# Branch gates of a streaming-encoder layer on a seven-product scheme, woven into the mixer

## The chip, the cores and the metric

The kernel runs on one core of one Trainium2 chip. A core has a matrix engine (TensorE, "PE"; "PEld" is its weight loading), a vector engine (VectorE, "DVE"), an activation engine (ScalarE, "ACT"), GpSimd ("POOL") and a queue that only issues transfers (SyncE, "SP"). Each works through its own list of instructions in order, and semaphores tie the lists together. The metric is the device time of one execution in microseconds.

## The reference, cut to what matters

One layer: a SwiGLU feed-forward part, a normalisation, a mixer, a normalisation, a second feed-forward part, a normalisation, and a gated embedding. There are 256 rows (positions) of 2048 channels, all float32. The change is in the mixer:

```python
proj = x @ w_in                                  # (256, 2048) @ (2048, 11272)
mq, mk, mv, mo, mi, mf, sq, sk, sv, ga, gb = _split_cols(proj)
...                                              # mLSTM branch -> y_m, stick-breaking branch -> y_sb
merged = sigmoid(ga) * (y_m @ w_up_m) + sigmoid(gb) * (y_sb @ w_up_sb)
return merged @ w_out
x = _layer_norm(ALPHA * x + mix, ln2_g, ln2_b)   # the residual x is needed again here
```

`ga` and `gb` are 2048 columns each. In blocks of 512 columns there are four pairs (ga block g, gb block g), g = 0 to 3.

## The kernel before, in words

**Products.** Float32 products are made of three reduced ones. Every weight tile of 256 rows by 512 columns ("raw") is loaded by SP's queue (line 997), rounded by ACT into a high part (line 1024), and DVE makes the low part as the difference (line 1028). Activations are kept transposed and split in the same way. A *unit* multiplies one weight tile by the activations of one half of the rows (128 positions): for each of two 128-row slices hi*hi, hi*lo and lo*hi (lines 1073 to 1075), so six matmuls of 512 columns. In the plain form (`group`) a weight tile serves two units, one for each half of the rows.

**The seven-product scheme** (`seven`, used by `up7` in both feed-forward parts). Two column blocks A and B with the same inputs, two halves of the rows and two halves of each 512-row chunk form 2 x 2 blocks, which are multiplied with seven products in place of eight, after Winograd's variant of Strassen's scheme. Each product needs a tile of its own, some of them sums of weight blocks. In the feed-forward parts one sum is made while loading, by an accumulating transfer on POOL's queue (line 1001), the others on DVE (line 310). The activations' sums ("forms") are made by `form_turn`. The results are combined on DVE (line 463). Products 1 and 2 run first (four units each); then for each of four chunks one unit of products 5, 7, 6, 4 and 3, so that these five accumulators are open together.

**Order of the work.** The program is one list of units, written by hand; `weave` mixes a side list evenly into a main list. A small planner keeps a clock that advances with each unit's six matmuls (0.2161 us each); all other work (transposes, normalisation, attention heads) are generators that are put into the engines' lists when their due time has come (`DELAY`). Loads and splits are put in ahead of the units: up to 8 raw tiles in the feed-forward parts and 5 in the mixer, and 6 split tiles (`limits`, `loads`, `split_one`, `splits_due`). In SBUF there is one pool of 44 pages of 4 KB per partition for everything large, and beside it the residual `xres` (two tiles of 8 KB per partition). In PSUM there are 8 banks, in one pool for accumulators ("mm") and for short-lived results ("ms").

**The mixer.** The columns of `w_in` come in groups: query, key, gates, value, output gate (mLSTM), then the 24 stick-breaking columns of 128 (`sb_columns`, six groups, the last with 256 columns), then the branch gates (`branch`, evicted by ACT with the sigmoid) and the up products (`ups`; DVE multiplies each result by its gate, line 861, and adds the two branches, line 864). Order: gates 0 and 1, ups 0 and 1, gates 2, ups 2, gates 3, ups 3. `merge_turn` transposes the merged result; those of g = 0 to 2 are due 1 to 6 us after the gates of 3.

**Stick-breaking heads** (`stick`). Eight heads run as two sequences, so that two heads go side by side, in four waves. Each head has three phases, and each of them takes a bank: scores (lines 791 on), cumulative sums (line 804, read by DVE in line 806), and the product with the values (line 814, read by ACT and DVE, lines 243 and 244). Between the phases are planner delays of 6.6 and 6.7 us (s0, s1) and of 5.0 us (s2).

Of the kernel before, what the change touches and what calls it, by code (L numbers as in the profile page):

```python
# [13 lines left out]
P = 128  # L14
# [11 lines left out]
PAGES = 44  # L26
# [3 lines left out]
RAW_FFN, RAW_MIX, RAW_EDGE = 8, 5, 4  # L30
SPLIT_FFN, SPLIT_MIX, SPLIT_EDGE = 6, 6, 11
# [14 lines left out]
    "alpha": 24.0, "form": 18.0, "ln_turn": 3.6, "ln_step": 2.1, "gb": 14.0, "h": 8.0, "silu": 6.0, "late": 9.0, "rest": 1.2, "mt": 3.2,  # L46
# [46 lines left out]
class ActT:  # L93


    def __init__(self, alloc, forms=None):
        self.alloc = alloc
        self.forms, self.whole = forms, {}
        self.tiles = {}
        self.left = {}  # L100
# [39 lines left out]
class Boundary:  # L140


    def __init__(self, mixer):
        self.mixer = mixer
# [25 lines left out]
def kernel(  # L170
# [12 lines left out]
    res_pool = ctx.enter_context(tc.tile_pool(name="res", bufs=1))  # L183
# [49 lines left out]
    xres = [res_pool.tile([P, D], F32, name=f"xres{t}") for t in range(TT)]  # L233

    def load_x(c, t):
        cs = slice(c * COL, (c + 1) * COL)
        nc.sync.dma_start(out=xres[t][:, cs], in_=x[t * P:(t + 1) * P, cs])
# [8 lines left out]
    def transposed(src, act, c, t):  # L246
# [5 lines left out]
        if act.forms:  # L252
# [5 lines left out]
        if act.forms and all(act.ready(c, h) for h in range(TT)):  # L258
            sched.spawn(form_turn(act, c), DELAY["form"] + 5.0 * c)
# [17 lines left out]


# [16 lines left out]
    def seven(wa, wb, rows, col0, cols, act, done):  # L295
# [19 lines left out]
        for m, sub in ((1, 0), (2, 2)):  # L315
            for i in range(n):
                units.append(unit(m, i, plain(rows_of(wa, (4 * i + sub) * P, col0, cols)), act, 0, sub))
        for i in range(n):
            b11, b12, b22, b21 = (rows_of(w, (4 * i + sub) * P, col0, cols)
                                  for w, sub in ((wa, 0), (wb, 0), (wb, 2), (wa, 2)))  # L320
            t1 = Raw(b12.src, cols, b11.src)
            t3, add = (Raw(b12.src, cols, b22.src), None) if i == n - 1 else (b12, plus(b12, b12, b22))
            first = Weight(t1, [t1], [])
            units += [
                unit(5, i, first, act.forms, 0, 0),
                unit(7, i, Weight(t3, [t3, b22], [t3], add), act.forms, 1, 0),
# [5 lines left out]

    program = []

    def boundary(mixer):
        program.append(Boundary(mixer))


    class Norm:
        def __init__(self, g, b, act, scale, wait):  # L340
            self.g_in, self.b_in, self.act, self.scale, self.wait = g, b, act, scale, wait
# [769 lines left out]
```

## Time and profile before

| what | value |
|---|---|
| median of 3 runs | 2207.58 us (2207.19 to 2207.64) |
| profiled execution | 2207.09 us |
| span of the profile | 2205.4 us |
| granted TensorE clock | 1.00 |
| busy, PE / DVE / ACT / POOL | 2196.6 / 1747.1 / 1244.5 / 118.9 us |
| read from memory | 539.90 MB |

How to read the rows shown below: in a row of a group the first number after the bar is the busy time in us, the second the mean duration of one in ns, and after the second bar stands the engine's idle time before these instructions with what ended it. Rows of instructions begin with start and duration in us. Rows of stretches give for each engine the busy time and the number of instructions, then the granted clock, the share of the DMA engines and GB/s. Matmuls are pipelined: their durations overlap, and the rate is read from their starts. The slices of the page are 55 us each: 0 to 12 are the first feed-forward part, 13 to 25 the mixer, 26 to 37 the second feed-forward part.

### The profile page before, as it was taken

The numbers are of one execution on the slowest core, as the hardware profiler recorded it, in microseconds if no ns is written. First come the engines' busy times: TensorE is split into PE (matmuls) and PEld (weight loads), VectorE is DVE, ScalarE is ACT, GpSimd is POOL, SyncE is SP. The second block draws the span as 40 slices with busy tenths as digits, with TensorE's granted clock in tenths as the row PEclk, the third lists the DMA queues.
The fourth block names the chain that finished last, engine by engine and source line by source line (L and its number), as shares of the span: only waits on it lengthen the run. The fifth ranks groups of instructions, "written<-read, shape, count | busy, mean of one in ns | idle before, by whom it ended". The sixth has DMA issues, their size and how long they took to land.

```text
span 2205.4 us, 27919 instructions
## 1 busy us (share of the span) xinstructions
PE 2196.6 (100%) x10062; PEld 1819.0 (82%) x10062; DVE 1747.1 (79%) x1923; ACT 1244.5 (56%) x1505; POOL 118.9 (5%) x111
## 2 busy tenths in 40 slices
PE   9999999999999999999999999999999999999999
PEld 7888888888888888888888888888888888887888
DVE  6999999999987874654445456699999999989774
ACT  7556656565655555545643344656565565656372
POOL 0100010000000000000100000000010001000000
PEclk9999999999999999999999999999999999999999
DMA  9899999999993765655566666579989999999553
GB/s 334 246 312 299 283 283 318 303 308 275 320 315 115 217 199 158 190 164 167 158 190 187 187 225 218 183 230 303 303 265 306 324 287 298 288 301 336 200 165 104
DMA packets 284811, 543.85 MB, mean 247 GB/s; under 512 B 17120, under 2 KB 26240, under 8 KB 284672
## 3 DMA queue, kind: packets, MB, share of 16 engines
q1 hardware_dynamic: 262912, 500.12, 68.3%
q0 software_dynamic: 21760, 41.95, 11.0%
q8 instruction: 79, 1.29, 0.2%
q14 instruction: 60, 0.49, 0.1%
HBM read 539.90 MB, written 2.10 MB: 246 GB/s over the span
## 4 chain that ended last, share of the span: by engine, by line
PE 94%; DVE 2%; DMA 2%; issue 1%; ACT 0%; SPq 0%; DVEq 0%; POOLq 0%; ACTq 0%
PE mm L1074 30%; PE mm L1073 30%; PE mm L1075 30%; DMA raw<-in_ffn_w_dram 2%; DVE split L1028 1%; PE ms L249 1%; PE ms L392 0%; DVE raw L310 0%; PE ms L791 0%; PE ms L814 0%; PE ms L742 0%; PE ms L754 0%; PE ms L804 0%; ACT split L1024 0%; DVE actT L256 0%
## 5 line engine op out<-in xcount | busy, mean ns | idle before, releaser
L1028 DVE TENSOR_TENSOR split<-raw,split 128x1024 fp32r<-128x1024 f32 (+1 forms) x1013 | 1177.6, 1201 | 237.8 <-ACT split L1024 225.3
L1024 ACT CAST split<-raw 128x1024 fp32r<-128x1024 f32 (+1 forms) x1013 | 1007.0, 1036 | 496.9 <-DVE raw L310 139.5
L1073 PE MATMUL mm<-split,actT 128*128 128x512 f32 (+2 forms) x3152 | 1226.9, 389 | 0.5 <-DVE xres L516 0.5
L1074 PE MATMUL mm<-split,actT 128*128 128x512 f32 (+2 forms) x3152 | 1215.1, 386 | 1.4 <-DVE split L1028 1.3
L1075 PE MATMUL mm<-split,actT 128*128 128x512 f32 (+2 forms) x3152 | 1215.1, 386 | 0.6 <-DVE actT L256 0.6
L1074 PEld LDWEIGHTS mm<-split,actT 128*128 128x128 f32 x3152 | 592.8, 188 | 120.3 <-DVE split L1028 6.1
L1075 PEld LDWEIGHTS mm<-split,actT 128*128 128x128 f32 x3152 | 592.2, 188 | 121.0 <-DVE actT L256 1.4
L1073 PEld LDWEIGHTS mm<-split,actT 128*128 128x128 f32 x3152 | 592.6, 188 | 117.0 <-issue 1.0
L310 DVE TENSOR_TENSOR raw<-raw 128x1024 f32<-128x1024 f32 x176 | 214.6, 1219 | 1.9
L1001 POOL DMA_DIRECT2D raw<-in_ffn_w_dram x80 | 95.9, 1198 | 1415.7 <-DMA raw<-in_ffn_w_dram 404.1
L251 ACT CAST actT<-ms 128x512 fp32r<-128x512 f32 x60 | 35.0, 585 | 89.4 <-PE ms L249 88.4
L463 DVE TENSOR_TENSOR temp<-mm,temp 128x512 f32<-128x512 f32 x112 | 76.7, 685 | 6.4 <-PE mm L1075 4.6
L516 DVE SCALAR_TENSOR_TENSOR xres<-mm,xres 128x512 f32<-128x512 f32 x96 | 65.3, 684 | 15.9 <-PE mm L1075 15.8
L256 DVE TENSOR_TENSOR actT<-ms,actT 128x512 fp32r<-128x512 f32 x60 | 40.9, 683 | 24.6 <-ACT actT L251 13.7
L221 ACT ACTIVATE big<-mm 128x512 f32<-128x512 f32 x20 | 12.0, 598 | 55.8 <-PE mm L1075 55.8
L221 ACT ACTIVATE temp<-temp 128x512 f32<-128x512 f32 (+1 forms) x48 | 28.5, 593 | 23.8 <-DVE temp L806 22.0
L221 ACT ACTIVATE temp<-mm 128x512 f32<-128x512 f32 (+1 forms) x22 | 12.3, 560 | 45.5 <-PE mm L1075 45.4
L217 ACT ACT_TABLE_LOAD x29 | 37.2, 1283 | 0.5
L244 DVE TENSOR_TENSOR actT<-temp,actT 128x512 fp32r<-128x512 f32 x32 | 21.4, 688 | 17.3 <-ACT actT L243 17.2
L861 DVE TENSOR_TENSOR big<-mm,big 128x512 f32<-128x512 f32 x16 | 11.1, 692 | 30.0 <-PE mm L1075 30.0
L690 DVE SCALAR_TENSOR_TENSOR temp<-ms,cw,temp 128x253 f32<-128x253 f32 (+2 forms) x48 | 23.1, 481 | 7.4 <-ACT temp L221 6.2
L221 ACT ACTIVATE rstd<-mv,eps 128x1 f32<-128x1 f32 x6 | 1.8, 295 | 46.4 <-DVE mv L375 46.4
(124 smaller groups left out, 542.1 us busy)
## 6 DMA issues: line engine op xcount, KB each, us to landing
raw<-in_ffn_w_dram SPq DMA_DIRECT2D x655, 512.0 KB, 6.5
raw<-in_w_in_dram SPq DMA_DIRECT2D x168, 512.0 KB, 3.8
raw<-in_ffn_w_dram POOLq DMA_DIRECT2D x80, 512.0 KB, 8.9
raw<-in_w_out_dram SPq DMA_DIRECT2D x32, 512.0 KB, 5.3
raw<-in_w_ple_gate_dram SPq DMA_DIRECT2D x24, 512.0 KB, 4.8
raw<-in_w_up_m_dram SPq DMA_DIRECT2D x16, 512.0 KB, 3.9
raw<-in_w_up_sb_dram SPq DMA_DIRECT2D x16, 512.0 KB, 4.4
raw<-in_w_ple_gate_dram SPq DMA_DIRECT2D x16, 256.0 KB, 4.4
```

The source lines that it names most:

```text
L217: nc.scalar.preload_act_table_set(table[0])
L221: nc.scalar.activation(out, in_, func, **kw)
L256: nc.vector.tensor_tensor(out=dst[:, 1], in0=ps[:], in1=dst[:, 0], op=ALU.subtract)
L310: nc.vector.tensor_tensor(out=out.tile[:, :, :cols], in0=a.tile[:, :, :cols], in1=b.tile[:, :, :cols], op=ALU.add)
L463: nc.vector.tensor_tensor(out=out, in0=a, in1=b, op=op)
L516: nc.vector.scalar_tensor_tensor(out=xs, in0=ps, scalar=0.5, in1=xs, op0=ALU.mult, op1=ALU.add)
L1001: nc.gpsimd.dma_start(out=r.tile[:, :, :r.cols], in_=r.plus, accum_op=ALU.add)
L1024: nc.scalar.copy(hi[:, ks], r[:, ks])
L1028: nc.vector.tensor_tensor(out=lo[:, ks], in0=r[:, ks], in1=hi[:, ks], op=ALU.subtract)
L1073: nc.tensor.matmul(ps, hi, w[0][:, k, :u.cols], start=first, stop=False)
L1074: nc.tensor.matmul(ps, hi, w[1][:, k, :u.cols], start=False, stop=False)
L1075: nc.tensor.matmul(ps, lo, w[0][:, k, :u.cols], start=False, stop=last)
```

## The change

Three of the four pairs of gate blocks (g = 1, 2, 3) are computed with the seven-product scheme instead of two plain groups. For these, no sum is made while loading: all weight sums are made on DVE. The 84 units of the three pairs are woven evenly into a main list of 128 units: the last stick-breaking columns (from column 14 on), the plain gates of g = 0, and the up products of g = 0, 1 and 2. The up products of g = 3 follow. The sums of the activations are made from the split parts that are there (hi + lo) while columns 10 to 13 are multiplied (`forms_later`). A gate's result is written to memory by ACT and DVE, combined on DVE (`both7`), and the sigmoid is applied in place, 1.5 planner us behind DVE's last operation. The sticks are spawned at the beginning of the woven list and wait for their columns.

To make room, the residual lies in four pages of the pool, which has 48 now. After the first normalisation SP writes it to a buffer in device memory (`put_away`, four transfers of 512 KB), and after the woven list it is read back into fresh pages (`bring_back`). In the woven list 7 raw tiles and 6 splits may be held ("wide"). Everything else of the diff is the same work under other names.

```diff
-PAGES = 44
+PAGES = 48
-RAW_FFN, RAW_MIX, RAW_EDGE = 8, 5, 4
-SPLIT_FFN, SPLIT_MIX, SPLIT_EDGE = 6, 6, 11
+HELD = {"ffn": (8, 6), "mix": (5, 6), "wide": (7, 6)}
+RAW_EDGE, SPLIT_EDGE = 4, 11
...
+    "alpha": 24.0, "away": 5.0, "sig": 1.5, "form": 18.0, ...
...
-    xres = [res_pool.tile([P, D], F32, name=f"xres{t}") for t in range(TT)]
+    res = {(t, k): big() for t in range(TT) for k in range(2)}
+    def xres(t, c0, n=COL):
+        return res[t, c0 // 1024][:, c0 % 1024:c0 % 1024 + n]
+    def put_away(t, k):
+        nc.sync.dma_start(out=away[t * P:(t + 1) * P, k * 1024:(k + 1) * 1024], in_=res.pop((t, k))[:])
+    def bring_back():
+        for k in range(2):
+            for t in range(TT):
+                res[t, k] = big()
+                nc.sync.dma_start(out=res[t, k][:], in_=away[t * P:(t + 1) * P, k * 1024:(k + 1) * 1024])
...
+    def forms_later(act, c):
+        act.whole[c] = big()
+        for t in range(TT):
+            hi, lo = (act.tiles[c, t][:, k].rearrange("q k s -> q (k s)") for k in range(2))
+            nc.vector.tensor_tensor(out=act.whole[c][:, t * COL:(t + 1) * COL], in0=hi, in1=lo, op=ALU.add)
+        yield 4.0
+        yield from form_turn(act, c)
...
-    def seven(wa, wb, rows, col0, cols, act, done):
+    def seven(wa, ca, wb, cb, rows, cols, act, done, loaded):
...
-            t1 = Raw(b12.src, cols, b11.src)
-            t3, add = (Raw(b12.src, cols, b22.src), None) if i == n - 1 else (b12, plus(b12, b12, b22))
-            first = Weight(t1, [t1], [])
+            if loaded:
+                t1 = Raw(b12.src, cols, b11.src)
+                first = Weight(t1, [t1], [])
+            else:
+                t1 = b11
+                first = Weight(t1, [b11, b12], [], plus(b11, b11, b12))
+            if loaded and i == n - 1:
+                third = Weight(t3 := Raw(b12.src, cols, b22.src), [t3, b22], [t3])
+            else:
+                third = Weight(b12, [b12, b22] if loaded else [b22], [b12], plus(b12, b12, b22))
...
+    def both7(w, ca, cb, act, dest, ready):
+        def put(k, t, a, b, op):
+            nc.vector.tensor_tensor(out=r[k, t], in0=a, in1=b, op=op)
+        def rest():
+            u = r[0, 1]
+            put(0, 1, held[7], u, ALU.add)
+            z = r[1, 1] = dest(1, 1)
+            nc.vector.scalar_tensor_tensor(out=z, in0=u, scalar=-1.0, in1=held[5],
+                                           op0=ALU.mult, op1=ALU.subtract)
+            ready(1, 1)
+        def done(m, ps):
+            held[m] = ps
+            if m == 1:
+                r[0, 1] = dest(0, 1)
+                nc.scalar.copy(r[0, 1], ps)
+            elif m == 2:
+                r[0, 0] = dest(0, 0)
+                put(0, 0, ps, r[0, 1], ALU.add)
+                ready(0, 0)
+            elif m == 6:
+                r[1, 0] = dest(1, 0)
+                put(0, 1, ps, r[0, 1], ALU.add)
+                put(1, 0, held[5], r[0, 1], ALU.add)
+                sched.spawn(rest(), DELAY["rest"])
+            elif m == 4:
+                sched.until(lambda: (1, 1) in r)
+                put(0, 1, ps, r[0, 1], ALU.add)
+                ready(0, 1)
+            elif m == 3:
+                put(1, 0, ps, r[1, 0], ALU.subtract)
+                ready(1, 0)
+        return seven(w, ca, w, cb, D, COL, act, done, False)
...
-    x1T = ActT(act_tile)
-    norm1 = Norm(ln1_g[0], ln1_b[0], x1T, None, (24.0, 3.0))
+    x1T = ActT(act_tile, ActT(act_tile), True)
+    norm1 = Norm(ln1_g[0], ln1_b[0], x1T, None, (24.0, 3.0), put_away)
...
+    program.extend(sb(2, 4) + sb(6, 4))
+    program.append(lambda: [sched.spawn(forms_later(x1T, c), 4.0 + 14.0 * c) for c in range(4)])
+    program.extend(sb(10, 4))
+    def sticks():
+        for a in (0, 1):
+            sched.spawn(in_sequence([stick(a), stick(a + 2), stick(a + 4), stick(a + 6)]))
...
-    program.extend(branch(0, 0) + branch(0, 1) + branch(1, 0) + branch(1, 1))
-    program.extend(ups(0) + ups(1))
-    program.extend(branch(2, 0) + branch(2, 1) + ups(2))
-    program.extend(branch(3, 0) + branch(3, 1))
+    def gate_ready(g):
+        def sigmoid(k, t):
+            a = gt[g, t][:, k * COL:(k + 1) * COL]
+            activate(a, a, ACT.Sigmoid)
+            flags.add(("gate", g, t, k))
+        return lambda k, t: sched.spawn(sigmoid(k, t), DELAY["sig"])
+    def pair(g):
+        return both7(w_in, ga0 + g * COL, ga0 + D + g * COL, x1T, gate_dest(g), gate_ready(g))
+    main = [sticks] + sb(14, 4) + sb(18, 4) + sb(22, 2) + branch(0, 0) + branch(0, 1) + ups(0) + ups(1) + ups(2)
+    mode("wide")
+    program.extend(weave(main, pair(1) + pair(2) + pair(3)))
+    mode("mix")
+    program.append(bring_back)
     program.append(lambda: [sched.spawn(merge_turn(g, t), 1.0 + 2.0 * g + t) for g in range(3) for t in range(TT)])
     program.extend(ups(3))
```

More of the change, by code (lines that the diff above doesn't have):

```diff
@@ L257, in transposed @@
         act.mark(c, t, 4)
-        if act.forms and all(act.ready(c, h) for h in range(TT)):
+        if act.soon and all(act.ready(c, h) for h in range(TT)):
             sched.spawn(form_turn(act, c), DELAY["form"] + 5.0 * c)
@@ L426, in affine @@
             self.whole.add((t, c))
+            if self.away and (t, c ^ 1) in self.whole:
+                sched.spawn(self.away(t, c // 2), DELAY["away"])
             return
@@ L855, in done @@
             activate(gt[g, t][:, half * COL:(half + 1) * COL], ps, ACT.Sigmoid)
+            flags.add(("gate", g, t, half))
         return done
@@ L859, in done @@
         def done(ps, t):
+            sched.until(lambda: ("gate", g, t, half) in flags)
             a = gt[g, t][:, half * COL:(half + 1) * COL]
```

102 lines of the change are left out of this document (58 added, 44 removed).

## The prediction

> **What bounds the kernel now.** I read the page's busy shares and slices first, then stretches of 50 to 600 us, then single instructions of TensorE (PE) and VectorE (DVE) around the place of the change.
>
> ```profile
> PE 2196.6 (100%) x10062; PEld 1819.0 (82%) x10062; DVE 1747.1 (79%) x1923; ACT 1244.5 (56%) x1505; POOL 118.9 (5%) x111
> DVE  6999999999987874654445456699999999989774
> PEclk9999999999999999999999999999999999999999
> PE 94%; DVE 2%; DMA 2%; issue 1%; ACT 0%; SPq 0%; DVEq 0%; POOLq 0%; ACTq 0%
> ```
>
> PE bounds every slice: it is on the chain of waits for 94%, at a full clock. DVE has room only in the mixer (slices 15 to 25, digits 4 to 6); in the two FFNs, where the seven-product scheme already runs, it stands at 9. So the question is what one matmul less is worth, and whether DVE can carry the scheme in the mixer too.
>
> ```profile
> core 0: us, PE busy (x) PEld busy (x) DVE busy (x) ACT busy (x) POOL busy (x), PEclk, DMA share, GB/s
> 50.00:650.00 600.00, 599.65 (x2681) 495.25 (x2680) 566.12 (x565) 360.51 (x384) 51.45 (x41) 1.00 0.96 298
> 950.00:1250.00 300.00, 300.00 (x1397) 250.08 (x1396) 147.29 (x166) 145.56 (x195) 10.50 (x16) 1.00 0.59 175
> 1460.00:2050.00 590.00, 588.47 (x2621) 483.84 (x2621) 553.86 (x545) 352.25 (x374) 46.90 (x39) 1.00 0.96 300
> ```
>
> The stretch that is changed (stick-breaking columns, branch gates, first up products) lies in 950:1250: DVE is busy 147 of 300 us. In the FFNs DVE is busy 566 of 600 and 554 of 590 us (94%) and DMA moves 298 GB/s, and still PE is idle for only 0.35 and 1.53 us.
>
> **The matmul saved.** Starts of TensorE in that stretch, first and last of 28 matmuls in a row:
>
> ```profile
> 1199.73 0.39 PE L1073 MATMUL mm<-split,actT 128*128 128x512 f32 x1
> ...
> 1205.85 0.39 PE L1073 MATMUL mm<-split,actT 128*128 128x512 f32 x1
> ```
>
> (1205.85 - 1199.73) / 27 = 0.2267 us per matmul; the 0.39 is latency, not rate. A unit (one 256-row weight tile against one half of the rows) is 6 matmuls, 1.360 us. A pair of plain gate groups is 2 x 8 tiles x 2 halves = 32 units; the scheme makes 7 products x 4 chunks = 28. Three pairs: 12 units, 72 matmuls, **-16.3 us**, all on the path.
>
> **DVE's added work.** Prices:
>
> ```profile
> 567.34 5.75 DVE L1028 TENSOR_TENSOR split<-raw,split 128x1024 fp32r<-128x1024 f32 x5
> 573.01 0.68 DVE L463 TENSOR_TENSOR temp<-temp 128x512 f32<-128x512 f32 x1
> 573.62 0.68 DVE L502 SCALAR_TENSOR_TENSOR temp<-temp 128x512 f32<-128x512 f32 x1
> L1028 DVE TENSOR_TENSOR split<-raw,split 128x1024 fp32r<-128x1024 f32 x979 | 1155.7, 1218 | 227.2 <-ACT split L1024 216.9 <-PE mm L1074 5.3 <-DMA raw<-in_w_in_dram 1.9
> L310 DVE TENSOR_TENSOR raw<-raw 128x1024 f32<-128x1024 f32 x176 | 214.6, 1219 | 1.9
> L1024 ACT CAST split<-raw 128x1024 fp32r<-128x1024 f32 x979 | 987.9, 1050 | 490.9 <-DVE raw L310 139.5 <-PE mm L1074 115.8 <-PE mm L1075 99.2
> ```
>
> A split takes 1.218 us, but five in a row take 5.75: (5.75 - 1.22) / 4 = 1.13 each, as ends overlap the next start; a 512-column operation advances 573.62 - 573.01 = 0.61. By these, L310 also counts 1.13. The scheme uses a weight tile once where the plain form uses it twice: 84 splits for 48, +36 x 1.13 = 40.7. Weight sums are all made on DVE here (in the FFN one is made by an accumulating DMA): 4 per chunk x 4 x 3 = 48 x 1.13 = 54.2. Combining results: 7 per pair, 21 x 0.61 = 12.8. Activation sums (forms_later): per chunk two adds, four half-width ones (half of 0.61) and two splits, 4 x (4 + 2) x 0.61 = 14.6, half of it before the stretch. With 147.3 that gives 147.3 + 40.7 + 54.2 + 12.8 + 7.3 = 262 us of DVE in 300 - 16.3 = 284 us of PE: 92%, just under the FFNs' 94%. ACT gets 36 x 1.05 = 38 us on 146 (65%). So DVE covers it on average; price of its late moments: FFN idle 0.35/600 to 1.53/590, so 0.2 to 0.7 us here; **+1**, since the last third (pair 3 beside the up products, which DVE must also multiply) is denser than the mean.
>
> The Trainium skill (VectorE: DVE Perf Modes, The DRAIN you can't avoid) says that the next operation does not start until the pipe is empty, which would make each split cost its full 1.22; the row of five in 5.75 does not agree. By that rule DVE would carry 262 x 1.218 / 1.13 = 282 of 284 us and the saving would be gone; by the row it fits.
>
> **PSUM.** There are 8 banks. The main stream holds 2, and in 20 of a pair's 28 units the side stream holds 5 (products 5, 7, 6, 4, 3 open together): one bank is left for everything else. Before, six were left while the sticks ran. Both sticks of a wave issue their matmuls at one moment and need two banks. In the weave 84 side units follow 128 main ones, 0.656 each. Planner time is 1.297 a unit, so the first wave starts after main unit 16 and its later phases (6.6 + 6.7, then 5.0) come 12 and 4 units on, at main 23 / side 15 and main 25 / side 17: pair 1 is in its 20 dense units (side 9 to 28). Waves 2 and 3 fall at pair 2's start or group changes, where banks are free; wave 4's last phase (main 65 / side 43) takes the two free banks just as the next accumulator is opened. Three places where PE must wait for a reader. How long a reader takes:
>
> ```profile
> 1019.48 0.81 PE L804 MATMUL ms<-temp,tri 128*128 128x384 f32 x2
> 1020.35 0.81 PE L804 MATMUL ms<-temp,tri 128*128 128x384 f32 x2
> 1020.55 0.55 DVE L806 TENSOR_TENSOR temp<-temp,ms 128x384 f32<-128x384 f32 x1 [5.34 <-PE ms L805]
> 1026.78 0.82 PE L814 MATMUL ms<-temp,big 128*128 128x256 f32 x4
> 1027.43 0.82 PE L791 MATMUL ms<-big 128*128 128x256 f32 x4
> 1028.56 0.29 DVE L244 TENSOR_TENSOR actT<-ms,actT 128x128 fp32r<-128x128 f32 x1 [0.33 <-ACT actT L243]
> 223.38 0.60 PE L249 MATMUL ms<-ident,temp 128*128 128x128 f32 x4
> 225.73 0.68 DVE L256 TENSOR_TENSOR actT<-ms,actT 128x512 fp32r<-128x512 f32 x1
> 1832.30 0.60 PE L249 MATMUL ms<-ident,temp 128*128 128x128 f32 x4
> 1840.12 0.68 DVE L256 TENSOR_TENSOR actT<-ms,actT 128x512 fp32r<-128x512 f32 x1
> ```
>
> With a quiet DVE: the second stick starts 0.87 after the first in L804, but would have to wait for 1020.55 + 0.55 = 1021.10, +0.75; in the last phase 0.65 turns into 1028.85 - 1026.78 = 2.07, +1.42; a third taker at 1.30 waits +0.77. Sum 2.9. With a loaded DVE a bank is held from 226.41 - 223.38 = 3.03 to 1840.80 - 1832.30 = 8.50 us: 1.0 to 6.4 longer than 2.07. At these places DVE has just come out of pair 1's light first units, so I take the 3.03 row: 2.9 + 3 x 1.0 = **+6**. Ends: 0 (a bank happens to be free) and 2.9 + 3 x 6.4 = 22.
>
> **Edits at no cost.**
>
> ```profile
> raw<-in_w_in_dram SPq DMA_DIRECT2D x168, 512.0 KB, 3.8
> SPq L997 <- PE mm L1075: 1246.7, 523, 13.1
> ```
>
> DMA: +24 loads; 132 loads of 0.524 MB in 284 us are 244 GB/s, below the FFNs' 298. Residual: 4 writes and 4 reads of 512 KB on SP's queue, each behind a DVE result or a freed page; SP waits on PE for its pages all the time anyway (523 waits, mean 2.4 us), 5 to 7 raw tiles and 6 splits lie ahead of PE, over 10 us, against 3.8 for a landing. If that cover were gone, 4 x 3.8 = 15 us, once, at the read back; but the residual is first needed 32 units (44 us) later. Pages: by my count the stretch wants 49 or 50 of 48, so a seventh raw waits a little on SP. Sticks are spawned earlier but poll the same flags; their results are wanted 40 units after they end. Sigmoids now run from memory after the combining, 1.5 planner us behind DVE's result; if DVE is late, ACT's next splits queue behind the sigmoid, 12 times for up to 5 us, but 6 splits (some 12 us of PE) lie ahead of PE; without that cover DVE, which waits for ACT, would lose the same time (the third rival). DVE's sums now wait for loads (b12, b22), with its combining behind them; a load is issued some 3 to 5 splits (6 to 10 us) before its sum, against 3.8. POOL gets no DMA: its queue holds the sticks' selects as before. The merge transposes of gate 2 now come 5 us behind its last up product instead of 32 units: PE may wait for a late DVE there, up to the 6.4 above; **+1**.
>
> **Sum.** 2207.09 (the profiled execution; 0.5 below the median of 2207.58) - 16.3 + 1 + 6 + 1 = 2198.8; against the median 2199.3. Predicted 2199.
>
> **Rivals.**
> - *Full saving.* The waves slip a unit or two and find banks: 2207.1 - 16.3 + 1 = 2192. For it: in 950:1250 PE is idle 0.00. Against: one bank cannot take two sticks.
> - *Bank waits at the FFN's longest holds* (slower). The same three places, holds of 8.5 instead of 3: 2207.1 - 16.3 + 22 + 2 = 2215. It decides from a sum of 14.3, a mean wait of 4.8. For it: the 1832.30 row. Against: the 223.38 row. The Trainium skill (TensorE: Matmul & The Clock Gate, Part 1) says that PE falls to half clock after about 3.4 us of idleness; no slice here shows a clock below 1.00, and no run here an idle time that long. By it, each such wait would add an estimated 1.7 us, 2220.
> - *DVE becomes the bound* in the last third: sums and splits arrive late and eat the saving, since DVE must wait for ACT too (216.9 us in all in the L1028 row). At 92% with the FFN's share of such waits it needs 262 / 0.944 = 278 of 284 us; 16 us more of waiting than that puts DVE 10 us past PE: 2207 - 16 + 10 + 8 = 2209, no change.
>
> **Chances.** Forecast (2195 to 2203) 0.46; full saving 0.20; DVE 0.14; bank waits 0.20. A measurement tells about 0.2% (4.4 us) from no change, so faster 0.66, same 0.14, slower 0.20. The range reaches down to the whole saving with nothing against it (2207.1 - 16.3 = 2190.8) and up to bank waits near their top, 2213.
>
> **What would show it.** Right: 72 fewer matmuls; 84 splits and 48 sums more or less evenly laid; DVE near 92% in the stretch; PE gaps at the second stick of wave 1 (L804 and L814 of before) of 2 to 3 us. Wrong: no gap there; DVE idle waiting for ACT while PE waits for splits; PE idle at the read back or at gate 2's transposes; the FFNs or the mixer's first half changing length.

## The result, and the profile after

The changed kernel takes 2227.98 us (median of 4 runs, 2221.34 to 2228.81), beside 2207.61 us for the kernel before on the same chip: ratio 1.0083, 95% interval 1.0062 to 1.0104. It is slower. The profiled execution took 2228.29 us, its span is 2226.6 us. The forecast was 2199 us, and 2227.98 lies above its range.

The lines of the code have new numbers in the changed kernel: the three matmuls of a unit are L1182 to L1184 (before L1073 to L1075), ACT's and DVE's parts of a split L1133 and L1137 (L1024, L1028), the weight sums L339 (L310). In a stick, the scores are L874, GpSimd's two selects L883 and L891 (L800 was the first), the cumulative sums L887 and L888, DVE's subtraction that reads their bank L889, the product with the values L897. L693 copies the transposed stick-breaking columns out of PSUM.

From the page of the changed kernel: busy times and two groups.

```profile
PE 2194.6 (99%) x9990; PEld 1812.0 (81%) x9990; DVE 1868.8 (84%) x2060; ACT 1289.8 (58%) x1555; POOL 133.9 (6%) x111
L339 DVE TENSOR_TENSOR raw<-raw 128x1024 f32<-128x1024 f32 x224 | 273.5, 1221 | 2.1
L883 POOL TENSOR_SCALAR_AFFINE_SELECT temp<-temp 128x256 f32<-128x256 f32 x8 | 21.2, 2666 | 191.1 <-DVE temp L882 191.1
```

PE executes 10062 - 9990 = 72 matmuls less, as the scheme should give. The weight sums are 224 - 176 = 48 more. DVE's busy time grew by 1868.8 - 1747.1 = 121.7 us. So the work is what the diff says, and yet the time grew. The row to stop at is the last: a select of GpSimd takes 2.67 us on average.

Where the time went can be read from the starts of PE's matmuls. From the mixer's first matmul to the first of the output projection the trace of before has 615.1 us and that of after 632.6 us: +17.5 where -16.3 were due, so 33.8 us were lost. The rest of the kernel hardly moved (first feed-forward part 700.3 and 702.8 us, from the output projection to the end 890.0 and 891.2). Within 950:1250, time between two starts beyond the rate of 0.227 us falls into three parts: waits behind full-size matmuls 20.2 us (before: 1.3), full-size matmuls at half clock 5.4 us, and 9.4 us more in the sticks' own small matmuls, where waits and half clock are both counted. 18.9 + 5.4 + 9.4 = 33.7.

Stretches of the changed kernel (length, then busy time and count of PE, PEld, DVE, ACT and POOL, the granted clock, DMA share, GB/s):

```profile
950.00:1250.00 300.00, 278.52 (x1248) 228.56 (x1247) 224.59 (x254) 175.07 (x228) 25.51 (x16) 0.95 0.63 191
1000.00:1050.00 50.00, 44.96 (x187) 35.87 (x186) 42.45 (x49) 29.64 (x39) 10.02 (x4) 0.93 0.51 156
1100.00:1150.00 50.00, 40.38 (x172) 31.91 (x170) 36.73 (x41) 36.05 (x53) 8.12 (x5) 0.92 0.58 168
```

Before, PE was busy for 300.00 of these 300 us at clock 1.00. Now it stands idle for 21.5 us, and for parts of the stretch the clock is halved. No engine is full over this stretch: DVE is busy 225 us, and in the 50 us in which PE loses most only 36.7. So this is latency, not the average load.

What PE waited for in the changed kernel between 950 and 1260 us (total us, how often, the longest):

```profile
PE ms L887 <- POOL temp L883: 7.6, 2, 6.1
PE mm L1182 <- ACT split L1133: 4.8, 1, 4.8
PE mm L1182 <- DVE big L693: 2.8, 1, 2.8
PE mm L1182 <- DVE actT L264: 2.1, 1, 2.1
```

The longest of them, in single instructions of PE, POOL, DVE and ACT (start and duration in us; in brackets the wait and what ended it):

```profile
1027.64 0.50 PE L1182 MATMUL mm<-split,actT 128*128 128x512 f32 x1 [2.83 <-DVE big L693]
1029.15 0.63 PE L1182 MATMUL mm<-split,actT 128*128 128x512 f32 x1
1029.58 0.63 PE L1183 MATMUL mm<-split,actT 128*128 128x512 f32 x1
...
1105.98 2.92 ACT L1133 CAST split<-raw 128x1024 fp32r<-128x1024 f32 x3
...
1144.74 1.02 DVE L882 SCALAR_TENSOR_TENSOR temp<-temp 128x384 f32<-128x384 f32 x2
1145.28 0.39 PE L1184 MATMUL mm<-split,actT 128*128 128x512 f32 x1
1145.43 7.62 POOL L883 TENSOR_SCALAR_AFFINE_SELECT temp<-temp 128x256 f32<-128x256 f32 x2 [19.10 <-DVE temp L882]
1145.68 1.22 DVE L339 TENSOR_TENSOR raw<-raw 128x1024 f32<-128x1024 f32 x1
1146.82 2.35 DVE L1137 TENSOR_TENSOR split<-raw,split 128x1024 fp32r<-128x1024 f32 x2
1149.09 1.22 DVE L339 TENSOR_TENSOR raw<-raw 128x1024 f32<-128x1024 f32 x1
1150.22 2.56 DVE L1137 TENSOR_TENSOR split<-raw,split 128x1024 fp32r<-128x1024 f32 x2
1151.76 1.65 PE L887 MATMUL ms<-temp,tri 128*128 128x384 f32 x2 [6.09 <-POOL temp L883]
1153.87 0.56 DVE L889 TENSOR_TENSOR temp<-temp,ms 128x384 f32<-128x384 f32 x1 [1.09 <-PE ms L888]
```

This is the second phase of the fourth wave. DVE makes the softplus terms of both sticks, GpSimd is to cut out their strict triangle, and PE is to sum them. The two selects begin at 1145.43, one behind the other, and end at 1151.71 and 1153.05, while DVE runs through sums and splits that were put in ahead, until 1152.78 and with a single gap, 0.09 us at 1151.44. PE's list has the cumulative sums next; behind them stand matmuls that run without a wait once the sums are done (from 1156.27 on). PE's matmuls stay in their order, and PE stands for 1151.76 - 1145.28 = 6.5 us. At the change from wave 2 to wave 3 it is ACT that is late (its splits start at 1105.98, after the sticks' activations), at 1024 a bank that DVE has not yet emptied.

GpSimd's first select in all eight uses, shortest, median and longest in ns, before and after:

```profile
L800 POOL TENSOR_SCALAR_AFFINE_SELECT temp<-temp x8: 580/730/1387, 1012.7 to 1090.5; 128x256 f32<-128x256 f32 x8
```

```profile
L883 POOL TENSOR_SCALAR_AFFINE_SELECT temp<-temp x8: 401/1386/8527, 1031.9 to 1151.7; 128x256 f32<-128x256 f32 x8
```

The instruction is the same; it takes 0.40 us where DVE leaves it room and up to 8.53 us where it does not. The Trainium skill (SBUF — State Buffer, "Who interferes with whom") says that a VectorE instruction with two inputs in SBUF and a GpSimd instruction that reads SBUF lock each other out. That agrees with the kind of work seen here: sums and splits have two such inputs. How long it lasts is shown by the trace: the first select at 1145.43 takes 6.28 us beside five sums and splits in a row and ends 0.27 us behind the fifth, which is the one with the gap behind it; the one of 8.53 us starts at 1031.95 and ends 0.26 us behind a row of seven.

Starts of matmuls also show the clock: 1029.58 - 1029.15 = 0.43 us from one to the next, against 0.227. In the clock record five stretches of the mixer are at half, 3.41, 3.41, 6.83, 10.24 and 3.41 us long, 27.3 us in all, each beginning near a wait or behind a row of short ones. The Trainium skill (TensorE: Matmul & The Clock Gate, Part 1) gives an idle window of about 3.4 us for the drop to half; the lengths here are multiples of 3.41 us and agree, but that a whole window must be idle is not what these runs show (last section).

### The profile page after: what moved, and what is told of

It reads as the page before. It is cut to its first block, busy times and chain, and to the rows that moved or that the text cites. A ratio compares the mean times of both kernels' runs of the same rounds, so it can differ in the third digit from the quotient of the medians.

```text
span 2226.6 us, 28148 instructions
## 1 busy us (share of the span) xinstructions
PE 2194.6 (99%) x9990; PEld 1812.0 (81%) x9990; DVE 1868.8 (84%) x2060; ACT 1289.8 (58%) x1555; POOL 133.9 (6%) x111
## 3 DMA queue, kind: packets, MB, share of 16 engines
q0 software_dynamic: 21760, 41.95, 10.9%
q8 instruction: 78, 1.28, 0.2%
## 5 line engine op out<-in xcount | busy, mean ns | idle before, releaser
L1137 DVE TENSOR_TENSOR split<-raw,split 128x1024 fp32r<-128x1024 f32 (+2 forms) x1049 | 1222.7, 1202 | 173.4 <-ACT split L1133 156.1
L1133 ACT CAST split<-raw 128x1024 fp32r<-128x1024 f32 (+2 forms) x1049 | 1043.7, 1036 | 520.6 <-DVE raw L339 176.7
L1182 PE MATMUL mm<-split,actT 128*128 128x512 f32 (+2 forms) x3128 | 1222.8, 391 | 11.1 <-ACT split L1133 4.8
L1184 PE MATMUL mm<-split,actT 128*128 128x512 f32 (+2 forms) x3128 | 1209.5, 387 | 0.6 <-DVE actT L276 0.6
L1182 PEld LDWEIGHTS mm<-split,actT 128*128 128x128 f32 x3128 | 590.2, 189 | 128.3 <-ACT split L1133 5.2
L1184 PEld LDWEIGHTS mm<-split,actT 128*128 128x128 f32 x3128 | 589.8, 189 | 120.2 <-DVE actT L276 1.5
L339 DVE TENSOR_TENSOR raw<-raw 128x1024 f32<-128x1024 f32 x224 | 273.5, 1221 | 2.1
L599 DVE SCALAR_TENSOR_TENSOR big<-mm,big 128x512 f32<-128x512 f32 x96 | 65.4, 685 | 15.4 <-PE mm L1184 15.2
L264 DVE TENSOR_TENSOR actT<-temp,actT 128x512 fp32r<-128x512 f32 x40 | 26.5, 688 | 17.9 <-ACT actT L263 17.9
L263 ACT CAST actT<-temp 128x512 fp32r<-128x512 f32 x40 | 24.1, 620 | 16.4 <-DVE temp L287 15.6
L883 POOL TENSOR_SCALAR_AFFINE_SELECT temp<-temp 128x256 f32<-128x256 f32 x8 | 21.2, 2666 | 191.1 <-DVE temp L882 191.1
```

The source lines that it names most:

```text
L339: nc.vector.tensor_tensor(out=out.tile[:, :, :cols], in0=a.tile[:, :, :cols], in1=b.tile[:, :, :cols], op=ALU.add)
L599: nc.vector.scalar_tensor_tensor(out=xs, in0=ps, scalar=0.5, in1=xs, op0=ALU.mult, op1=ALU.add)
L1133: nc.scalar.copy(hi[:, ks], r[:, ks])
L1137: nc.vector.tensor_tensor(out=lo[:, ks], in0=r[:, ks], in1=hi[:, ks], op=ALU.subtract)
L1182: nc.tensor.matmul(ps, hi, w[0][:, k, :u.cols], start=first, stop=False)
L1184: nc.tensor.matmul(ps, lo, w[0][:, k, :u.cols], start=False, stop=last)
```

## Experiments

Theory A, from the rows above: the select on GpSimd, shut out by a loaded DVE, is the cause. Rival B: any step of the stick chains is late, since each of their operations stands in order behind the splits and sums that were put in ahead; take away one wait, and the next takes its place. Later, two more questions were open: is it the number of pairs or the place of the dense work, and can delays or shorter lists mend it. Each kernel ran beside the kernel before, whose median was 2207.6 to 2209.8 us in these runs; "mixer" is again the time from the mixer's first matmul to the first of the output projection in its trace (615.1 before, 632.6 after).

| run | median us | ratio to before (95%) | mixer us |
|---|---|---|---|
| the change | 2227.98 | 1.0083 (1.0062 to 1.0104) | 632.6 |
| e1_mask_dve | 2226.17 | 1.0073 (1.0058 to 1.0088) | 631.8 |
| e2_raw6 | 2226.69 | 1.0076 (1.0060 to 1.0091) | 632.7 |
| e3_stagger_raw6 | 2214.29 | 1.0019 (1.0009 to 1.0029) | 618.0 |
| e4_two_pairs | 2198.08 | 0.9950 (0.9934 to 0.9967) | 604.3 |
| e5_act_frees_bank | 2226.14 | 1.0075 (1.0061 to 1.0088) | 629.6 |
| e6_residual_only | 2209.81 | 1.0001 (0.9992 to 1.0010) | 615.1 |
| e7_masks_stagger | 2217.16 | 1.0036 (1.0022 to 1.0050) | 623.2 |
| e8_three_pairs_late | 2215.72 | 1.0028 (1.0016 to 1.0039) | 621.7 |
| e9_two_pairs_with_sticks | 2222.88 | 1.0062 (1.0047 to 1.0077) | 628.7 |
| e10_four_splits | 2221.77 | 1.0060 (1.0045 to 1.0075) | 627.0 |
| e11_four_splits_later | 2212.08 | 1.0013 (1.0003 to 1.0022) | 617.1 |
| e12_three_pairs_patient | 2207.92 | 0.9995 (0.9986 to 1.0004) | 615.1 |

### The select on DVE

```diff
+    strict = consts.tile([P, P], F32, name="strict")
+    nc.gpsimd.affine_select(strict[:], ones[:], pattern=[[1, P]], compare_op=ALU.is_gt,
+                            fill=0.0, base=0, channel_multiplier=-1)
...
-        nc.gpsimd.affine_select(diag(sp), diag(sp), pattern=[[0, 2], [1, P]], compare_op=ALU.is_gt,
-                                fill=0.0, base=0, channel_multiplier=-1)
+        for o in (0, 2 * P):
+            nc.vector.tensor_tensor(out=sp[:, o:o + P], in0=sp[:, o:o + P], in1=strict[:], op=ALU.mult)
```

> The changed kernel (2228.0 us) with one edit: the first triangular select of each stick (GpSimd) becomes two multiplications by a mask on VectorE, 16 operations of some 0.2 us, 3 us of VectorE in all. Theory A (TensorE stands in front of the sticks' own instructions: GpSimd's selects are held up by VectorE, 1.6 and 6.3 us of waits, and the half clock after them costs 4 to 5 us more): 2215 to 2218, no TensorE wait of 6 us left, fewer half-clock stretches. Theory B (the woven scheme is too dense for VectorE and ScalarE whatever the sticks do): 2228 or slower, since VectorE gets more work.

Measured 2226.17 us, mixer 631.8: almost nothing gained. PE's longest wait in that kernel (its lines from the sticks on have numbers higher by four):

```profile
PE ms L891 <- DVE temp L893: 9.1, 2, 7.3
```

No wait for GpSimd is left, and the time is the same. In the place of the 6.1 us stands one of 7.3 us: the second stick's cumulative sums wait for a bank, which the first stick's subtraction (L893) frees, and this stands in DVE's list behind the same splits and sums. Theory A alone falls.

### A control, and the sticks of a wave apart

The second needs a raw tile less for its pages, so the first shows what that alone does.

```diff
-HELD = {"ffn": (8, 6), "mix": (5, 6), "wide": (7, 6)}
+HELD = {"ffn": (8, 6), "mix": (5, 6), "wide": (6, 6)}
```

> The changed kernel with 6 raw tiles held in the woven list where it has 7 (control for the next run, and a test of the pages). Theory A: within 2 us of 2228. Theory B, or loads that come too late: 4 us slower or more, with VectorE waiting for transfers.

Measured 2226.69 us and a mixer of 632.7: the seventh raw tile is worth nothing.

```diff
-HELD = {"ffn": (8, 6), "mix": (5, 6), "wide": (7, 6)}
+HELD = {"ffn": (8, 6), "mix": (5, 6), "wide": (6, 6)}
...
+        if h in (1, 3):          # the second sequence starts 4 planner us later
+            yield 4.0
```

> As the run before with 6 raw tiles, and the second stick of the first two waves starts 4 planner us after the first, so that two sticks no longer ask for two PSUM banks at one moment. Theory A: of some 10 us of waits for banks about half go, the selects stay late: 5 to 8 us below the run before. Theory B: equal to the run before within 2 us.

Measured 2214.29 us: -12.4 against the control, more than expected. PE's waits (lines from the sticks on are higher by two: L885 and L893 are the selects):

```profile
PE ms L899 <- POOL temp L893: 3.6, 2, 2.9
PE ms L889 <- POOL temp L885: 3.0, 2, 2.7
```

With the sticks of a wave apart they no longer ask for two banks at one moment, and the longest wait for the first select falls from 6.1 to 2.7 us. That two phases met is thus a good part of the loss, 12 of 34 us, as far as one run shows it: the later start also puts every step elsewhere in DVE's list.

### The pairs moved behind the sticks

```diff
-    main = [sticks] + sb(14, 4) + sb(18, 4) + sb(22, 2) + branch(0, 0) + branch(0, 1) + ups(0) + ups(1) + ups(2)
+    program.extend([sticks] + sb(14, 4) + sb(18, 4) + sb(22, 2) + branch(0, 0) + branch(0, 1))
+    main = branch(1, 0) + branch(1, 1) + ups(0) + ups(1) + ups(2)
     mode("wide")
-    program.extend(weave(main, pair(1) + pair(2) + pair(3)))
+    program.extend(weave(main, pair(2) + pair(3)))
```

Only two pairs are on the scheme here; the sticks run beside plain units, as before the change.

> Stick-breaking columns and the plain gates 0 run unwoven, then two pairs (2 and 3) are woven between the plain gates 1 and the up products; so the sticks are out of the dense part, and 8 units (10.9 us) are saved where the change saves 12. Theory A: 2207.6 - 10.9 + 1 to 2 = 2198, clock 1.00. Theory B: TensorE waits for splits in the woven part (0.7 side units for each main unit, as in the change), 2205 or slower.

Measured 2198.08 us, ratio 0.9950: faster than the kernel before, and the mixer is 604.3 us, -10.8; two pairs should save 48 x 0.2267 = 10.9. Stretches of that kernel:

```profile
950.00:1250.00 300.00, 300.00 (x1398) 250.05 (x1397) 215.74 (x244) 173.06 (x226) 11.18 (x16) 1.00 0.63 202
1250.00:1300.00 50.00, 50.00 (x234) 41.53 (x233) 48.66 (x54) 30.70 (x36) 0.00 (x0) 1.00 0.84 284
```

PE is never idle, and the clock is full. DVE is busy for 48.66 of 50 us, 97%, and keeps up: here a VectorE that is nearly full does no harm, as the sticks' steps no longer stand in its list.

### The bank emptied by ACT

e1's mask, 6 raw tiles, and

```diff
-        nc.vector.tensor_tensor(out=z[:, n], in0=z[:, n], in1=ps[:], op=ALU.subtract)
+        activate(sp[:, n], ps[:], ACT.Copy)
+        nc.vector.tensor_tensor(out=z[:, n], in0=z[:, n], in1=sp[:, n], op=ALU.subtract)
```

> Mask on VectorE as in e1, 6 raw tiles, and the cumulative sums of a stick are copied out of PSUM by ScalarE before VectorE subtracts them, so that the bank is freed by ScalarE and not by VectorE's queue. Theory A (the bank is held because its only reader stands in VectorE's queue): the wait of 7.5 us before the second stick's cumulative sum in e1 falls to 1 to 3 us, and a half-clock stretch of 3 to 7 us goes with it: 2226.2 - 5 - 2 = 2219, the other waits stay. Rival (not the bank: the stick's data or the splits are late): the wait stays at 5 us or more under another name and the time within 2 us of e1.

Measured 2226.14 us. The wait keeps its length and changes its name; PE's wait, and two instructions of ACT in that kernel:

```profile
PE ms L891 <- ACT big L225: 7.3, 1, 7.3
```

```profile
1148.64 2.13 ACT L1138 CAST split<-raw 128x1024 fp32r<-128x1024 f32 x2 [3.21 <-DVE raw L343]
...
1154.33 0.60 ACT L225 ACTIVATE big<-mm 128x512 f32<-128x512 f32 x1 [2.25 <-DVE split L1142]
```

The bank that was wanted is now held by a plain gate's accumulator, whose sigmoid on ACT stands behind splits that wait for DVE's sums. ACT has time (180 of 300 us busy), but its list is tied to DVE's. This speaks for the rival B named at the head of this section.

### The residual alone

All gates in plain groups in the old order; the residual's pages, its write and its read back stay.

```diff
-    main = [sticks] + sb(14, 4) + ... + ups(2)
-    mode("wide")
-    program.extend(weave(main, pair(1) + pair(2) + pair(3)))
+    program.extend([sticks] + sb(14, 4) + sb(18, 4) + sb(22, 2) + branch(0, 0) + branch(0, 1) + branch(1, 0) + branch(1, 1))
+    program.extend(ups(0) + ups(1))
+    program.extend(branch(2, 0) + branch(2, 1) + ups(2))
+    program.extend(branch(3, 0) + branch(3, 1))
```

> All gates plain and in the order of before, no sums of activations; only the residual is in the pool's pages (48 of them), written away and read back. Theory A (it is free): 2207.6 within 2 us, mixer 615 us long as before. Rival (it costs): the first feed-forward part 2.5 us longer as in the changed kernel, or TensorE idle at the read back: 2210 or more.

Measured 2209.81 us beside 2209.78: 1.0001 (0.9992 to 1.0010), and a mixer of 615.1 us. In the time of the kernel the residual in memory costs nothing that can be told from zero, and in the mixer nothing. One sign of the rival is there: the first feed-forward part of this trace takes 705.0 us, 700.3 before and 701.3 to 704.6 in the other changed kernels. With one trace of the kernel before, whether the pages or the run make this difference stays open.

### Both selects on DVE, and the sticks apart

e3 and e1's mask together, and the second select (L891) by the mask too.

> e3 (second stick 4 planner us later, 6 raw tiles; 2214.3) with both selects of a stick made on VectorE. Theory A (GpSimd's delay was hidden behind the wait for the bank in e1, so that it only shows once the banks are apart): the 6.6 us of waits for GpSimd in e3 go, minus 4 to 8: 2206 to 2210. Rival (GpSimd's delay is only another face of VectorE's queue): the same 6 us are then waited for VectorE, 2213 to 2215.

Measured 2217.16 us, 2.9 above e3. PE's longest wait (L903 is the product with the values, L898 the mask in place of the second select):

```profile
PE ms L903 <- DVE temp L898: 4.7, 2, 3.5
```

Even with the sticks apart GpSimd is not the point: as work of DVE, the selects join the list that makes everything late.

### Three pairs behind the sticks' columns

```diff
+    program.extend([sticks] + sb(14, 4) + sb(18, 4) + sb(22, 2) + branch(0, 0))
-    main = [sticks] + sb(14, 4) + ... + ups(2)
+    main = branch(0, 1) + ups(0) + ups(1) + ups(2)
...
-        return seven(w, ca, w, cb, D, COL, act, done, False)
+        return seven(w, ca, w, cb, D, COL, act, done, True)
```

with e7's masks and stagger. Some of the weight sums are made while loading.

> All three pairs, woven only from the second half of gate 0 on (64 main and 84 side units, 1.3 side for each main), with five of the 16 sums of a pair made by accumulating transfers as in the feed-forward part, staggered sticks and masks on VectorE. Theory A (with the sticks mostly out of the dense units and VectorE at some 96% the saving comes through): 2207.6 - 16.3 + 3 to 6 = 2195 to 2198. Theory B (this density is too much for VectorE; TensorE waits for splits): 2205 or slower.

Measured 2215.72 us, mixer 621.7. PE's waits:

```profile
PE ms L903 <- DVE temp L898: 7.0, 2, 4.7
PE mm L1190 <- DVE split L1144: 6.2, 9, 1.9
```

The last steps of the sticks still reach into the woven part (7.0 us), and a new wait comes in, nine times, for DVE's splits. That DVE is full is not what the trace shows: in 1150:1300 it is busy for 135.1 of 150 us, 90%, less than in e4 at its fullest. The DMA engines are busy for 95% of that time, and between 1110 and 1310 us ACT's splits wait for loads, which they do in e4 nowhere in that stretch:

```profile
ACT split L1140 <- DMA raw<-in_w_in_dram: 23.0, 7, 5.2
```

So the later place has a limit of its own, and e4's two pairs keep below it; whether loads or DVE's list set it was not separated.

### Two pairs beside the sticks

```diff
-    main = [sticks] + sb(14, 4) + sb(18, 4) + sb(22, 2) + branch(0, 0) + branch(0, 1) + ups(0) + ups(1) + ups(2)
+    main = [sticks] + sb(14, 4) + sb(18, 4) + sb(22, 2) + branch(0, 0) + branch(0, 1)
     mode("wide")
-    program.extend(weave(main, pair(1) + pair(2) + pair(3)))
+    program.extend(weave(main, pair(2) + pair(3)))
     mode("mix")
+    program.extend(branch(1, 0) + branch(1, 1) + ups(0) + ups(1) + ups(2))
```

with 6 raw tiles: e4's two pairs, about as densely woven, at the old place.

> The same two pairs as in e4 (8 units, 10.9 us saved) at the same density of 0.7 side units for each main unit, but woven where the change has them, beside the stick-breaking columns, the sticks and the plain gates 0 (6 raw tiles); gates 1 and the up products run unwoven after them. Theory A (the place beside the sticks costs, not the number of pairs or their density): the waits of the four waves come back, 18 to 30 us: 2215 to 2227, with half-clock stretches. Theory B (three pairs were too much for VectorE, two are not): 2198 as e4.

Measured 2222.88 us, 24.8 above e4 (mixers 628.7 and 604.3). A stretch, and PE's waits:

```profile
950.00:1250.00 300.00, 284.91 (x1290) 234.32 (x1289) 215.87 (x245) 175.66 (x232) 22.29 (x16) 0.97 0.62 199
```

```profile
PE ms L887 <- POOL temp L883: 5.3, 2, 4.3
PE ms L687 <- DVE big L693: 3.2, 1, 3.2
```

DVE is busy for 215.87 us here and for 215.74 in e4, in the same 300 us. So the same average load costs PE 15 us of idleness in one place and none in the other. While sticks run it is not the same, as 1000:1100 shows, first in this kernel, then in e4:

```profile
1000.00:1100.00 100.00, 94.42 (x460) 78.82 (x459) 80.91 (x95) 65.55 (x96) 8.14 (x8) 0.97 0.59 191
1000.00:1100.00 100.00, 100.00 (x505) 84.42 (x504) 52.92 (x73) 64.92 (x105) 10.36 (x14) 1.00 0.54 169
```

This is the run that decides: neither the number of pairs nor DVE's average load, but that the sticks run beside them. Whether the sticks then lack DVE's time or the banks that the pairs hold, it can't tell, as both come with the pairs.

### A shorter list, and more time between the phases

```diff
-HELD = {"ffn": (8, 6), "mix": (5, 6), "wide": (7, 6)}
+HELD = {"ffn": (8, 6), "mix": (5, 6), "wide": (7, 4)}
```

> The changed kernel with 4 split tiles made ahead in the woven list instead of 6. Theory A (a stick's operations stand behind the splits and sums that were put into VectorE's queue ahead of them, some 1.1 us each): the queue is 2 splits and their sums shorter, the longest waits fall from 6 to 7 us to 3 to 5: 2214 to 2222. Theory B (TensorE lacks splits): more waits for splits, 2232 or slower.

Measured 2221.77 us. PE's waits:

```profile
PE mm L1182 <- ACT split L1133: 5.7, 4, 1.9
PE mm L1183 <- DVE split L1137: 4.7, 8, 0.8
PE ms L887 <- POOL temp L883: 1.6, 1, 1.6
```

With four splits ahead instead of six, the wait for the select falls from 7.6 to 1.6 us in sum, as a shorter list should make it. But the store of splits is also what bridges late moments, and PE now waits for splits, 10.4 us. So of what the shorter list gains a good part is given back: the time falls by 6 us, of 34 that were lost.

```diff
+HELD = {"ffn": (8, 6), "mix": (5, 6), "wide": (7, 4)}
-    ... "s0": 6.6, "s1": 6.7, "s2": 5.0,
+    ... "s0": 6.6, "s1": 12.0, "s2": 5.0,
```

> As e10, and the second phase of each stick comes 12 planner us after the first VectorE operation instead of 6.7. Theory A: the first stick's data are there when TensorE comes to them, so the waits for GpSimd's select go (some 5 us), the second stick's wait for the bank stays: 3 to 6 us below e10. Rival (the wait only moves to the next thing that stands in the same queue): within 2 us of e10.

Measured 2212.08 us, -9.7 against e10, more than either theory said. A stretch, and PE's waits:

```profile
950.00:1250.00 300.00, 286.67 (x1317) 234.90 (x1316) 238.69 (x268) 181.91 (x236) 25.91 (x16) 1.00 0.65 206
```

```profile
PE mm L1183 <- DVE split L1137: 4.5, 7, 1.5
PE ms L897 <- DVE actT L264: 4.1, 3, 1.6
PE ms L887 <- POOL temp L883: 0.4, 1, 0.4
```

The clock is 1.00: no wait is over 1.9 us from start to start, and no stretch at half is left. From e10 to e11 PE's waits in this stretch fell from 17.1 to 9.4 us, and the 4.2 us that e10 loses to half clock are gone; the sticks' own matmuls take 1.7 us more. That is 10.2 us, beside 9.9 us of mixer.

```diff
+HELD = {"ffn": (8, 6), "mix": (5, 6), "wide": (6, 5)}
+    ... "s0": 6.6, "s1": 12.0, "s2": 8.0,
...
+        if h in (1, 3):
+            yield 4.0
```

> All three pairs in the place of the change, with what e3, e10 and e11 did together: the second stick of the first two waves 4 planner us later, 12 planner us in place of 6.7 before the second phase and 8 in place of 5 before the third, 5 splits and 6 raw tiles held in the woven list. Theory A (what was lost is waits of the sticks' instructions behind VectorE's queue and for one free bank, and each can be had back by time between them): 2202 to 2208, clock 1.00, waits of 5 us or less in all beside those for splits. Rival (below some point the waits only change their name, as in e7): 2210 or more.

Measured 2207.92 us, ratio 0.9995 (0.9986 to 1.0004): three pairs beside the sticks without a loss, and without a gain. A stretch, and PE's waits:

```profile
950.00:1250.00 300.00, 291.16 (x1325) 241.08 (x1325) 242.87 (x273) 183.45 (x239) 27.72 (x16) 0.98 0.67 206
```

```profile
PE ms L876 <- DVE actT L264: 3.7, 1, 3.7
PE ms L687 <- DVE big L693: 3.1, 1, 3.1
```

The time is at the upper end of theory A's range, but its conditions are not met: the clock falls three times, and PE's waits come to 8.8 us, none of them for splits. Against the change, 17.5 us of mixer are back, by things that make the sticks less urgent or DVE's list shorter; GpSimd is busy as long as in the changed kernel (27.72 and 25.51 us), but PE waits for other things. DVE is at its fullest of the kernels shown in this stretch, so here a higher average load goes with a shorter time. What is left are mostly other readers in DVE's list. Not tried: the longer delays alone, with 7 raw tiles and 6 splits.

## Why the prediction was wrong

**Right.** The saving itself: 72 matmuls, and 10.8 us for the 48 of e4 against 10.9 by the same rate. DVE's added work: 40.7 + 54.2 + 12.8 + 14.6 = 122.3 us were forecast, 121.7 measured. That DVE covers it on average: e4 runs at 97% of DVE without a wait of PE, so the +1 for its late moments was if anything too much, and that each split costs its full 1.22 is not what these runs show: at 1146.82 two splits take 2.35 us. The section that the prediction cites for that (the Trainium skill, VectorE: DVE Perf Modes, The DRAIN you can't avoid) also says that a next operation that is not held starts earlier, so the rows need not contradict it. The 92% for the stretch did not come, however: DVE is busy for 75% of 950:1250, as PE stands still there and the woven work runs on past 1300. The residual, its transfers and the pages: free in the median (e6). The seventh raw tile: nothing (e2). The direction of the slower rival: waits of the sticks at the holds of a loaded DVE; its 2215 and 2220 fell short of 2228.

**The step that failed** is "PSUM, +6": "Three places where PE must wait for a reader", at the holds of a DVE that "has just come out of pair 1's light first units". The three places are there, and about as long as said (starts of PE in the changed kernel): 1.9 and 1.0 us from 1038.7 on, 1.7 us at 1051.0, and 1.1 and 2.4 us from 1163.5 on. That is 8.0 us from start to start and 6.9 beyond the rate, in place of 6, though at the first it was the select that came last and not a bank's reader. But these are the smaller part. Not in the sum were 6.5 us at 1145.3 and 1.2 us at 1153.4 (the fourth wave's second phase, where the prediction had no conflict), 5.2 and 1.3 us at 1101.9 (the change of waves 2 and 3, "where banks are free"), and 3.2 us at 1024.4 (the transposed columns). By what ended them, six of these ten waits are for the reader of a bank (10.5 us from start to start) and four for data that are late (14.8 us). The prediction counted places where two steps want the last bank. What was to be counted are the steps of a chain that goes PE, ACT, DVE, GpSimd, PE several times, each of which now stands behind a list of some 7 us: from 1145.68 to 1152.78 DVE worked on what had been put in ahead. With delays of 6.7 and 5.0 planner us between phases, the rounds of waves 1 and 4 come too late, bank or not (the second and third phases of waves 2 and 3 cost PE no wait of 0.9 us or more, as the prediction had it), and whatever PE finds first in its list gives the wait its name. e1, e5 and e7 show this: three times the name changed, and the time fell by less than 2 us or rose.

**A sentence that failed with it:** "POOL gets no DMA: its queue holds the sticks' selects as before". The queue was as before, but not the duration: 0.40 to 8.53 us. What shares an engine's list was looked at, what shares its access was not. Yet e1 shows that this alone decides nothing: with the first select on DVE the time is the same.

**The clock** was put beside the slower rival as an aside, at 1.7 us for a wait. Measured were 27.3 us at half in the changed kernel, which cost 5.4 us at the full-size matmuls alone. As the waits were to be short, it had no part in the sum. But two of the five falls, at 1042.8 and 1169.1, stand behind waits at the places that were forecast, of 1.9 and 1.0 us and of 2.4 us: even the forecast's own waits were long enough.

**"DVE becomes the bound in the last third"** is not what happened: the 33.8 us lie in 950:1250, with PE's last long wait at 1165.2, and nothing was lost in the third pair's part behind it, though DVE is full there:

```profile
1250.00:1300.00 50.00, 50.00 (x222) 41.41 (x222) 49.86 (x49) 28.63 (x30) 0.00 (x0) 1.00 0.85 275
```

Nor did PE wait at gate 2's transposes, for which the other +1 stood. Waits for DVE's splits come where the pairs are pressed together beside few plain units (e8), with late loads as a second possible reason.

The 9.4 us in the sticks' own matmuls can be shared out from the same starts: the five waits that begin there (1.0, 1.7, 1.2, 1.1 and 2.4 us) make 6.2 us beyond the rate, and half clock in the cumulative sums (0.86 us from the first start to the last for a stick at full clock, 1.28, 1.65 and 1.62 us at 1042.4, 1151.8 and 1154.6) makes 2.0. What is open: how much of the loss is the lack of banks and how much DVE's list. e3, e10 and e11 each change the times of both.

## What to carry to other kernels

Before a dense stream is put beside a chain of short steps, ask how long an instruction of the chain stands in each list it passes, and compare that with the time the order of work gives it; an average load of 75 or 92% says nothing on it. In this kernel a scheme that trades matmuls for work on another engine belongs where no chain of short steps uses that engine: two pairs there gained 0.5%, the same two beside the attention lost 0.6%. And when a wait vanishes and the time stays, look for its next name before the next mend.

## What the runs showed of the hardware

GpSimd's select of 128x256 values took 0.40 us beside a quiet VectorE. In the changed kernel one took 6.28 us beside five sums and splits that followed one another without a gap, and one 8.53 us beside seven: it did not get in between two of them. It is not always so. The select at 1114.24 ran beside a sum, ended 0.27 us behind it after 1.39 us, and the split behind that sum took 1.42 us instead of 1.22. What tells these cases apart was not found.

The clock falls to half at shorter waits than expected: in e3 a stretch of 3.41 us at half began at 1027.3, behind a wait of 2.2 us that had begun at 1024.8. Nor is the length of the wait all that counts: e10 and e11 have the same row of waits there (1.76, 1.26 and 0.53 us, from 1022.5 and from 1023.4 on), and e10 falls to half at 1026.8 while e11 does not. What tells them apart is where the waits lie. In all fourteen traces the changes of the clock in a run are whole multiples of 3.413 us apart, so a run can be cut into steps of that length. The step in front of a fall, in the changed kernel and in e10, and the step of e11 with the least work:

```profile
1025.69:1029.10 3.41, 1.46 (x6) 1.24 (x7) 3.41 (x5) 2.01 (x3) 0.00 (x0) 1.00 0.09 35
1023.36:1026.77 3.41, 1.71 (x6) 1.05 (x6) 2.49 (x3) 3.41 (x4) 0.00 (x0) 1.00 0.24 64
1021.67:1025.09 3.42, 1.98 (x11) 1.43 (x9) 1.78 (x3) 2.95 (x6) 0.00 (x0) 1.00 0.48 153
```

PE is idle for 1.95, 1.70 and 1.44 us of them. Counted over all fourteen traces without their first 30 and last 60 us, the steps in front of the 30 falls hold from 1.7 to 3.4 us of idle PE, 29 of them 1.9 or more, and no step at full clock without a fall behind it holds more than 1.83. So in these runs PE fell to half at the end of a step of which about half was idle. That is also why the drop can come after work has begun again: in the changed kernel the wait ends at 1027.64 and the step at 1029.1, so that the half clock slows the matmuls that follow.
